# Stores of a hybrid recurrent layer issued from ScalarE's DMA queue instead of SyncE's

## The chip, the cores and the metric

One core of a Trainium2 chip. The metric is the device time of one execution, in microseconds (us). Engines are called as in the profile: PE is TensorE (PEld its weight loads), DVE is VectorE, ACT is ScalarE, POOL is GpSimd, SP is SyncE, which computes nothing and issues DMAs. A DMA is issued by an instruction in an engine's queue, and that queue runs in order: an issue that waits holds up everything behind it on its engine. SPq in the profile is SP's queue.

## What is computed

One layer of a decoder with four groups of recurrent heads, all in float32: 2048 prompt tokens with 16 learned tokens in front, and 8 sample sequences of 4 tokens, which start from their own states.

```python
def _layer(x, st, lw, lb, prefix):
    u = jnp.einsum('btd,de->bte', x, lw['w_in'])             # 1024 -> 3340 columns
    (z_a, xbc, dt_raw, z_b, u_b, z_c, qkv, b_raw, a_raw,
     z_d, q_d, f_d, i_d) = _split_last(u, _IN_SIZES)
    xbc, c_ssd_new = _causal_conv(xbc, c_ssd, ...); xbc = jax.nn.silu(xbc)
    y, s_ssd_new = _with_prefix(_ssd_chunked, (xs, dt, a, bm, cm), s_ssd, prefix, SSD_CHUNK)
    y_a = _rms_heads(y + d * xs, ...) * jax.nn.silu(z_a)       # A: Mamba-2 SSD
    y5, s5r_new, s5i_new = _s5_scan(u_b, ...)                # B: complex diagonal scan
    y_b = glu(jax.nn.gelu(y5)) * jax.nn.silu(z_b)
    qkv, c_gdn_new = _causal_conv(qkv, c_gdn, ...); qkv = jax.nn.silu(qkv)
    o, s_gdn_new = _with_prefix(_gdn_chunked, (l2norm(q), l2norm(k), v, beta, g), s_gdn, ...)
    y_c = _rms_heads(o, ...) * jax.nn.silu(z_c)              # C: gated delta rule
    o, s_hg_new = _with_prefix(_hgrn_chunked, (silu(q_d), k_h, i_d, logf), s_hg, ...)
    y_d = _rms_heads(o, ...) * jax.nn.silu(z_d)              # D: HGRN2
    out = jnp.einsum('btc,cd->btd', concat(y_a, y_b, y_c, y_d), lw['w_out'])
    return _layernorm(DN_ALPHA * x + out, lw['ln_g'], lw['ln_b']), states
```

The input x goes through a layer norm first. Outputs are the layer's y of prompt and samples and the seven final states of each.

## The kernel before

The 2096 tokens are 17 chunks: chunk 0 holds the 16 learned tokens and the 32 sample tokens, the others 128 prompt tokens each. The projections run over two halves (chunks 0 to 8 and 9 to 16) in blocks of up to 384 or 512 tokens. A product in float32 accuracy is three: high part times high part, high times low, low times high (xh and xl, the two halves of w).

- `phase1a` (one per half): layer norm and transposition of x into xh and xl, and the products that are wanted token-major: u of branch B, and i (the values of branch D) with the gates' inputs. A result goes from PSUM (pj) into a tile zs by ACT (L88 in the profile is a helper through which ACT's and DVE's operations of this phase go), and a DMA stores it to u_d or v_d (L463).
- `phase1b` runs through `proj`: some 25 weight tiles of 128 columns for each half. `wload` (L578 to 580) loads one tile into wr, ACT makes the high part of w (L579) and POOL the low part. Each block of products is taken up by the tile's consumer. `conv_tile` copies it to raw (L635), forms the causal convolution cv on POOL and DVE (L639, L641) and its SiLU on ACT (L652), in a tile acc that is normalised later, or in a tile zs that is stored at once to qkv_d or xbc_d (L654). `stream_out` has ACT write a function of the block to zs (L813 to L827) and stores it to z_d (the gates z) or qfk_d (q, f and k of branch D) at L804.
- zs has two buffers, shared by all of these; pj has two buffers in PSUM, pq, for all other products, six. raw, cdec and the other tiles have theirs.
- All else are jobs, generators that `poll` weaves between the products: the gates (g_g, L521; te, dtte), the conv tiles' l2 norm (sq, L681 to L683; l2r), `c_pre` with its decays (rows_d is loaded into cdec, POOL subtracts at L725, ACT exponentiates at L727, DVE multiplies into cma at L753), the constants of branch B (cosT, sinT, bui, L956 to L961; bs_wt, the sum of L1070 and L1071 at L1072; bs_cl loaded at L1042), and `d_group` of branch D, whose output is copied by ACT to d_oy (d_oya, d_oyb; L1703) and stored to od_d (L1704).
- Behind the second half's tiles come the chunks of branches C and A (a_L is the decay of A, L725 to L727), `rms` (f_sq, L1752; f_h), and for every chunk the gating and the product with w_out (woh and wol are its high and low parts, L1816 and L1817), the closing layer norm and the store of y.

The order of PE's instructions is the one in which the kernel is written out, with the jobs woven in by fixed times. On the other engines a scheduler orders the instructions by its own model of the times, except in a few chains that are kept in order. It also gives every DMA one of eight completion semaphores (DMAHW0 to DMAHW7) in rotation, in the order of issue over all queues; a DMA waits until the one before it on its semaphore has landed. In the kernel before all 1047 DMAs are issued by SP: `self.ld` for loads and `self.st` for stores are the same function, `nc.sync.dma_start`.

Of the kernel before, what the change touches and what calls it, by code (L numbers as in the profile page):

```python
# [62 lines left out]
def tof(t):  # L63
    return HEAD + 128 * (t - 1) if t else 0
# [6 lines left out]
class Pinned:  # L71
    """An engine whose instructions don't move ahead of earlier ones."""
# [8 lines left out]
class Chain:  # L81
    """An engine whose instructions issued through here stay in the order in which they are written."""
# [14 lines left out]
class Kern:  # L97
# [8 lines left out]

    def pool(self, name, bufs, **kw):
        return self.tc.tile_pool(name=name, bufs=bufs, reuse_waits="tile", **kw)

    # The tensor engine runs in the order in which the kernel is written out. Dependent chains  # L110
    # are generators ("jobs") that yield the time until their next step can start; they are
    # woven between the matrix products of the projections.
# [64 lines left out]
    # ---------------------------------------------------------------- constants  # L177
    def consts(self, cp):
        nc, V, S, G = self.nc, self.V, self.S, self.G
        a = self.a  # L180
# [13 lines left out]
        # sums the two parts of 32 channels of a head  # L194
# [24 lines left out]
    # ---------------------------------------------------------------- phase 1  # L219
    def small_loads(self, cp):  # L220
        """Job: small parameters, and the conv histories of the sample sequences channel-major."""
        a, V = self.a, self.Vp
        yield 8.2
        # channel-major small parameters, through one transpose
# [29 lines left out]
        # HGRN2 lower bound: softmax over the single layer, cumulative sum minus the first entry  # L254
# [70 lines left out]
    def phase1a(self, half, xp):  # L325
        """Layer norm and transposition of the input, and the products whose results are wanted token-major.
        The first yield comes before anything that needs the space of xh, xl or the weight ring."""
# [46 lines left out]
        def weights(i, parts):  # L374
            """u | i, dt, a, b: high and low parts."""
# [23 lines left out]
        else:  # L399
            # the first tile waits for as little as possible: one row comes by DMA, the other through the tensor engine  # L400
# [35 lines left out]
        for q, j in sorted(((q, j) for q in range(len(seq)) for j in (0, 1)), key=lambda x: x[0] + lag * (x[1] != half)):  # L436
# [26 lines left out]
            self.st((self.v_d if j else self.u_d)[tof(t):tof(t) + n], uv[:n, 0:256])  # L463
# [18 lines left out]
    def gates_in(self, half, sp):  # L482
# [3 lines left out]
        o = 1 - half          # chunk 0, the tail, is the first of half 0  # L486
# [14 lines left out]
        # softplus = max(x, 0) + log1p(e), log1p(e) = 2 atanh(e / (2 + e))  # L501
# [20 lines left out]
        # beta = sigmoid  # L522
# [1627 lines left out]
```

## Time and profile before

| | |
|---|---|
| time, three runs | 1446.28, 1452.7, 1456.98 us; median 1452.7 |
| profiled execution: span (its only time) | 1448.2 us |
| granted clock of PE, mean | 0.936 of full speed |
| PE busy | 1294.9 us, 89% |
| DVE, ACT, POOL busy | 934.2, 536.1, 616.3 us |
| DMA traffic | 195.79 MB, 135 GB/s in the mean |

The busy times are sums over the whole span, and the stages differ: a stretch is read in the table by stretch, and what an engine waited for in its list of waits. PEclk is the clock that was granted to TensorE, 1.00 at 2.4 GHz and 0.5 at 1.2 GHz; a mean between them is a mix of the two. A line number is that of the kernel before; in the changed kernel all lines from 107 on are two further down.

### The profile page before, as it was taken

The numbers are of one execution on the slowest core, as the hardware profiler recorded it, in microseconds if no ns is written. First come the engines' busy times: TensorE is split into PE (matmuls) and PEld (weight loads), VectorE is DVE, ScalarE is ACT, GpSimd is POOL, SyncE is SP. The second block draws the span as 40 slices with busy tenths as digits, with TensorE's granted clock in tenths as the row PEclk, the third lists the DMA queues.
The fourth block names the chain that finished last, engine by engine and source line by source line (L and its number), as shares of the span: only waits on it lengthen the run. The fifth ranks groups of instructions, "written<-read, shape, count | busy, mean of one in ns | idle before, by whom it ended". The sixth has DMA issues, their size and how long they took to land. (4 is left out here: it accounts for less than half of the span.)

```text
span 1448.2 us, 23800 instructions
## 1 busy us (share of the span) xinstructions
PE 1294.9 (89%) x8596; PEld 1090.3 (75%) x8596; DVE 934.2 (65%) x2173; ACT 536.1 (37%) x1010; POOL 616.3 (43%) x508
## 2 busy tenths in 40 slices
PE   7984898899898999998996888789997999999997
PEld 6974788878877999877674677677775677777776
DVE  8899524557978549474355789962345676665654
ACT  3224256545214342353543442242434332333211
POOL 4065322524433312152434443441324476676665
PEclk9997999999989999999998899899998899999999
DMA  8511552464337434215534633125649777676333
GB/s 211 192 49 36 127 143 57 140 189 114 106 97 203 145 104 153 77 39 158 157 87 121 201 102 95 44 88 145 177 124 251 196 198 190 198 182 184 111 105 113
DMA packets 259007, 195.79 MB, mean 135 GB/s; under 512 B 70950, under 2 KB 231928, under 8 KB 258873
## 3 DMA queue, kind: packets, MB, share of 16 engines
q1 hardware_dynamic: 258890, 194.28, 47.2%
q8 instruction: 68, 1.11, 0.3%
q14 instruction: 49, 0.39, 0.1%
HBM read 125.01 MB, written 64.31 MB: 131 GB/s over the span
## 5 line engine op out<-in xcount | busy, mean ns | idle before, releaser
L126 PE MATMUL pj<-xh,w 128*128 128x384 f32 (+2 forms) x1760 | 547.8, 379 | 10.8 <-ACT raw L635 5.5
L126 PEld LDWEIGHTS pj<-xh,w 128*128 128x128 f32 x1760 | 339.7, 200 | 57.4 <-issue 11.6
L126 PE MATMUL pj<-xl,w 128*128 128x384 f32 (+2 forms) x880 | 322.8, 367 | 0.0
L126 PEld LDWEIGHTS pj<-xl,w 128*128 128x128 f32 x880 | 176.3, 200 | 12.4 <-issue 0.5
L580 POOL TENSOR_TENSOR w<-wr,w 128x1024 fp32r<-128x1024 f32 x44 | 109.9, 2497 | 85.6 <-ACT w L579 68.0
L641 DVE SCALAR_TENSOR_TENSOR cv<-raw,par,cv 128x384 f32<-128x384 f32 (+2 forms) x150 | 130.5, 872 | 9.5 <-POOL cv L639 8.2
L126 PE MATMUL pj<-woh,o_mh 128*128 128x512 f32 (+2 forms) x280 | 116.6, 416 | 6.3 <-DVE xt L1846 3.2
L126 PE MATMUL pj<-wol,o_mh 128*128 128x512 f32 (+2 forms) x280 | 109.4, 391 | 6.2 <-POOL wol L1817 5.9
L126 PE MATMUL pj<-woh,o_ml 128*128 128x512 f32 (+2 forms) x280 | 109.4, 391 | 0.0
L126 PE MATMUL pj<-w,xh 128*128 128x256 f32 (+3 forms) x544 | 105.2, 295 | 0.0
L639 POOL TENSOR_SCALAR cv<-raw,par 128x384 f32<-128x384 f32 (+2 forms) x50 | 49.3, 986 | 119.0 <-ACT raw L635 95.4
L126 PEld LDWEIGHTS pj<-w,xh 128*128 128x128 f32 (+1 forms) x544 | 84.6, 189 | 1.2 <-ACT xh L88 0.8
L126 PE MATMUL pj<-w,xl 128*128 128x256 f32 (+3 forms) x272 | 78.0, 291 | 0.8 <-DVE xl L88 0.8
L725 POOL TENSOR_TENSOR cdec<-cdec,negm 128x256 f32<-128x256 f32 x32 | 29.4, 921 | 98.6 <-DMA cdec<-rows_d 63.1
L126 PEld LDWEIGHTS pj<-woh,o_mh 128*128 128x128 f32 (+1 forms) x280 | 52.3, 187 | 18.6 <-DVE xt L1846 4.0
L126 PEld LDWEIGHTS pj<-wol,o_mh 128*128 128x128 f32 (+1 forms) x280 | 52.5, 188 | 16.0 <-POOL wol L1817 6.9
L1789 DVE TENSOR_TENSOR y<-y,f_R 128x768 f32<-128x768 f32 (+1 forms) x17 | 27.1, 1591 | 56.0 <-POOL f_R L1788 50.9
L126 PEld LDWEIGHTS pj<-woh,o_ml 128*128 128x128 f32 (+1 forms) x280 | 52.2, 187 | 12.3 <-issue 0.7
L308 POOL TENSOR_TENSOR lnrs<-lnve,mhalf 128x1 f32<-128x1 f32 (+1 forms) x34 | 24.5, 720 | 74.0 <-DVE lnve L88 46.2
L813 ACT ACTIVATE zs<-pj 128x384 f32<-128x384 f32 (+2 forms) x40 | 20.8, 520 | 87.6 <-PE pj L126 72.8
L126 PEld LDWEIGHTS pj<-w,xl 128*128 128x128 f32 (+1 forms) x272 | 51.2, 190 | 1.5 <-DVE xl L88 1.3
L1788 POOL TENSOR_TENSOR f_R<-f_R,f_z 128x768 f32<-128x768 f32 (+1 forms) x17 | 30.2, 1778 | 51.1 <-DMA f_R<-r_d 32.5
(570 smaller groups left out, 2687.8 us busy)
## 6 DMA issues: line engine op xcount, KB each, us to landing
wr<-in_w_in_dram SPq DMA_DIRECT2D x46, 512.0 KB
xt<-in_x_prompt_dram SPq DMA_DIRECT2D x16, 512.0 KB
xn_d<-xt SPq DMA_DIRECT2D x16, 512.0 KB
ma<-cma SPq DMA_DIRECT2D x64, 128.0 KB
xt<-xn_d SPq DMA_DIRECT2D x16, 512.0 KB
out_dram<-xt SPq DMA_DIRECT2D x15, 512.0 KB
f_R<-r_d SPq DMA_DIRECT2D x32, 192.0 KB
cdec<-rows_d SPq DMA_DIRECT2D x32, 128.0 KB
```

Of the source, the lines that this page charges most:

```text
L126: self._pe(self.PE.matmul(out, lhsT, rhs, start=start, stop=stop, **kw), 0.01 + n * (1 if rhs.dtype == F32R else 4) / 2400)
L308: self.G.tensor_tensor(rs[:n], ve[:n], self.mhalf[:n, 0:1], ALU.pow)
L580: self.G.tensor_tensor(w[:, :, 1], raw, w[:, :, 0].bitcast(F32), SUB)
L639: G.tensor_scalar(cv[:, 0:m], raw[:, 3:3 + m], w[3], b, op0=MUL, op1=ADD)
L641: V.scalar_tensor_tensor(cv[:, 0:m], raw[:, k:k + m], w[k], cv[:, 0:m], op0=MUL, op1=ADD)
L725: G.tensor_tensor(d[:n, :, :n], d[:n, :, :n], m[:n, None, :n].to_broadcast([n, nh, n]), ADD)
L813: S.activation(z, p, AF.Silu)
L1788: G.tensor_tensor(R[:, :, :n], R[:, :, :n], z[:, :, :n], MUL)
L1789: V.tensor_tensor(y6[:, 0:6, :n], y6[:, 0:6, :n], R[:, :, :n], MUL)
```

## The change

A third function, `self.sa`, is ScalarE's `dma_start`. It takes the place of `self.st` at the stores of tiles that an ACT instruction wrote last. (The other lines of the diff remove comments.)

```diff
         self.ld = nc.sync.dma_start
         self.st = nc.sync.dma_start
 
+        self.sa = nc.scalar.dma_start
+
     def pool(self, name, bufs, **kw):
...
             S.copy(uv[:n, 0:256], p[:n, 0:256])
             if j:
                 V.tensor_copy(self.gat[:n, t, :], p[:n, 256:268])
-            self.st((self.v_d if j else self.u_d)[tof(t):tof(t) + n], uv[:n, 0:256])
+            self.sa((self.v_d if j else self.u_d)[tof(t):tof(t) + n], uv[:n, 0:256])
             if q == len(seq) - 1:
...
                 S.activation(o, cv[:, 0:n], AF.Silu)
             if nrm is None:
-                self.st(dst[:, t0:t0 + n], o)
+                self.sa(dst[:, t0:t0 + n], o)
             else:
...
             for fn, dst in outs:
                 z = self.zp.tile([128, 512], F32, name="zs")
                 fn(z[:, 0:n], p[:, 0:n])
-                self.st(dst[:, t0:t0 + n], z[:, 0:n])
+                self.sa(dst[:, t0:t0 + n], z[:, 0:n])
             if mark and t0 + n == BASE[self.half] + WID[self.half]:
...
                 oy = tp.tile([128, 2, 128], F32, name="d_oy" + sfx)
                 S.copy(oy[:, :, :n], ov[:, :, :n])
-                self.st(self.od_d[:, :, tof(t):tof(t) + n].rearrange("g p t -> p g t"), oy[:, :, :n])
+                self.sa(self.od_d[:, :, tof(t):tof(t) + n].rearrange("g p t -> p g t"), oy[:, :, :n])
                 p = self.pt()
```

These are 34 stores of u_d and v_d, 30 of qkv_d and xbc_d out of zs, 70 of z_d and qfk_d, and 16 of od_d: 150 of 1047 DMAs. 897 stay on SP, among them all loads and the stores of tiles that DVE, POOL or PE wrote last, and one of od_d for chunk 0. The bytes and the shapes are the same. ACT has as many computations as before, with the 150 issues among them; each store stands behind ACT's own write of its tile. The order on PE doesn't change at all. The scheduler places some instructions of the other engines anew: on ACT 91 of 1012 by up to 5 places, on DVE 597 by up to 17, on POOL 22 by up to 4, and of the DMAs left on SP 113 by up to 10.

**Phase 1a, SP's queue and ACT's.** Before, the stores at L463 stand on SP between loads (bs_cl, wr, x); in brackets what each waits for (Activation, DVE, PE and Pool are those engines' own progress):

```order
L271 DMA aco<-in_gdn_a_log_dram 128x4 [waits DMAHW1_49]
L271 DMA sd_691<-in_ssd_d_dram 128x4 [waits DMAHW2_49]
L1042 DMA bs_cl<-in_s_c_re_dram 128x2x64 [waits DMAHW3_49]
L1042 DMA bs_cl<-in_s_c_im_dram 128x2x64 [waits DMAHW4_49]
L463 DMA u_d<-zs 48x256 [waits DMAHW5_49,Activation_49]
L1105 DMA gluw<-in_s_glu_w_dram 128x2x256 [waits DMAHW6_49,Pool_49]
L578 DMA wr<-in_w_in_dram 128x8x128 [waits DMAHW7_49,PE_49]
L372 DMA xn_d<-xt 128x1024 [waits DMAHW0_49,DVE_49]
L339 DMA xt<-in_x_prompt_dram 128x1024 [waits DMAHW1_49,DMAHW0_49,PE_49]
L463 DMA v_d<-zs 128x256 [waits DMAHW2_49,Activation_49]
```

Now, on ACT, they stand behind the copy to zs and ahead of the next copies and of xh, the high part of x, which PE multiplies with:

```order
L88 COPY zs<-pj 128x256 [waits PE_49]
L465 DMA u_d<-zs 128x256 [waits DMAHW4_49,Activation_49]
L88 CAST xh<-pq 128x4x48 [waits PE_49] x2
L88 COPY zs<-pj 48x256 [waits PE_49]
L465 DMA u_d<-zs 48x256 [waits DMAHW6_49,Activation_49]
L88 CAST xh<-pq 128x4x128 [waits PE_49] x2
L88 COPY zs<-pj 128x256 [waits DMAHW4_49,PE_49]
L465 DMA v_d<-zs 128x256 [waits DMAHW2_49,Activation_49]
L88 COPY zs<-pj 128x256 [waits DMAHW6_49,PE_49]
L465 DMA u_d<-zs 128x256 [waits DMAHW5_49,Activation_49]
```

The u_d and v_d stores have left SP, and with them the wait for ACT in front of wr and x; on ACT they bring waits for DMAHW semaphores.

**ACT at about 100 us.** Before, the square of the l2 norm (sq, L682) stands twice ahead of raw and of the high part of a weight tile:

```order
L650 ACTIVATE acc<-cv 128x256
L682 ACTIVATE sq<-sq 128x64
L682 ACTIVATE sq<-sq 128x256
L635 COPY raw<-pj 128x384
L579 CAST w_1491<-wr 128x8x128
```

Now raw and the weights stand between the two squares:

```order
L652 ACTIVATE acc<-cv 128x256
L684 ACTIVATE sq<-sq 128x64
L637 COPY raw<-pj 128x384
L581 CAST w_1491<-wr 128x8x128
L684 ACTIVATE sq<-sq 128x256
```

raw (L637 now) and w (L581 now) have moved one square forward.

**DVE at about 140 us.** Before, four steps of the rotation cosT, sinT (L957, L959) stand ahead of the third sum bs_wt (L1072), which PE transposes next:

```order
L1070 TENSOR_TENSOR bs_wt<-bs_X,bpr 128x128
L957 TENSOR_TENSOR bs_l<-sinT,bui 128x256
L959 TENSOR_TENSOR sinT<-cosT,bui 128x16x16 x2
L957 TENSOR_TENSOR bm_1371<-bui 128x16
L959 TENSOR_TENSOR bvi<-bur,bui 128x16
L571 COPY g_rs<-pq 16x128
L641 SCALAR_TENSOR_TENSOR cv<-raw,par,cv 128x384
L626 COPY raw<-hist 128x8x3
L627 MEMSET raw 128x3
L1072 TENSOR_TENSOR bs_wt<-bs_wt,bs_wu 128x512
```

Now the sum comes first and the four steps (L959 and L961 in the new numbers) behind it:

```order
L958 TENSOR_TENSOR bvr<-bur 128x16
L573 COPY g_rs<-pq 16x128
L643 SCALAR_TENSOR_TENSOR cv<-raw,par,cv 128x384
L1074 TENSOR_TENSOR bs_wt<-bs_wt,bs_wu 128x512
L628 COPY raw<-hist 128x8x3
L629 MEMSET raw 128x3
L959 TENSOR_TENSOR bs_l<-sinT,bui 128x256
L961 TENSOR_TENSOR sinT<-cosT,bui 128x16x16 x2
L959 TENSOR_TENSOR bm_1371<-bui 128x16
L961 TENSOR_TENSOR bvi<-bur,bui 128x16
```

The steps L957 and L959 of before have moved behind the sum; the conv step cv in front of it is the same.

**ACT at about 1100 us.** Before, the square f_sq of `rms` stands behind three of four exponentials of a_L:

```order
L813 ACTIVATE zs<-pj 128x512
L815 ACTIVATE zs<-zs,par 128x512
L727 ACT_TABLE_LOAD
L727 ACTIVATE a_L<-a_L,nac 128x128 x3
L1752 ACTIVATE f_sq<-f_sq 128x768
L727 ACTIVATE a_L<-a_L,nac 128x128
```

Now it stands ahead of them and of the load of their function table, behind the store of the gate:

```order
L815 ACTIVATE zs<-pj 128x512
L817 ACTIVATE zs<-zs,par 128x512
L806 DMA z_d<-zs 128x512
L1754 ACTIVATE f_sq<-f_sq 128x768
L729 ACT_TABLE_LOAD
L729 ACTIVATE a_L<-a_L,nac 128x128 x4
```

f_sq (L1754 now) comes next in the after order, with no a_L in front of it.

## Rows read from the trace of the kernel before

**Rows 1.** Page: busy us of each engine (share of the span) and instructions

```profile
PE 1294.9 (89%) x8596; PEld 1090.3 (75%) x8596; DVE 934.2 (65%) x2173; ACT 536.1 (37%) x1010; POOL 616.3 (43%) x508
```

**Rows 2.** Table by stretch: length, busy us (instructions) PE PEld DVE ACT POOL, PEclk, DMA share, GB/s

```profile
50.00:100.00 50.00, 46.41 (x358) 45.27 (x356) 47.60 (x230) 15.41 (x34) 17.79 (x26) 1.00 0.34 114
100.00:150.00 50.00, 26.82 (x144) 24.09 (x142) 48.27 (x148) 20.94 (x41) 30.10 (x33) 0.80 0.11 29
```

**Rows 3.** PE's waits: waiting line, what ended it: us in total, times, longest us

```profile
PE pq L120 <- DVE bs_wt L1072: 13.3, 3, 8.3
...
PE pq L126 <- ACT Qa L1635: 6.3, 5, 2.6
...
PE pj L126 <- ACT raw L635: 5.5, 2, 3.1
...
PE pq L120 <- DMA bs_cl<-in_s_c_re_dram: 2.3, 1, 2.3
```

**Rows 4.** SP's waits, same columns, at the four kinds of store

```profile
SPq L654 <- ACT zs L652: 80.7, 16, 10.5
...
SPq L463 <- ACT zs L88: 42.8, 18, 5.6
...
SPq L804 <- ACT zs L815: 37.6, 15, 5.5
...
SPq L1704 <- ACT d_oya L1703: 22.2, 9, 3.5
```

**Rows 5.** Page, costliest groups: count | busy us, mean ns | idle before, releaser

```profile
L126 PE MATMUL pj<-xh,w 128*128 128x384 f32 (+2 forms) x1760 | 547.8, 379 | 10.8 <-ACT raw L635 5.5
...
L725 POOL TENSOR_TENSOR cdec<-cdec,negm 128x256 f32<-128x256 f32 x32 | 29.4, 921 | 98.6 <-DMA cdec<-rows_d 63.1
```

**Rows 6.** Issues of two kinds of store: duration ns min/median/max, first and last start

```profile
L463 SPq DMA_DIRECT2D u_d<-zs x17: 319/330/457, 22.4 to 608.0; - x17
...
L804 SPq DMA_DIRECT2D qfk_d<-zs x30: 319/376/1328, 184.6 to 814.6; - x30
```

**Rows 7.** ACT's waits, columns as in rows 3

```profile
ACT zs L813 <- PE pj L126: 72.8, 27, 7.5
```

**Rows 8.** SP's waits for a DMA that the issue doesn't need

```profile
SPq L578 <- DMA wr<-in_w_in_dram: 8.4, 3, 3.4
...
SPq L463 <- DMA xt<-in_x_prompt_dram: 1.9, 1, 1.9
```

**Rows 9.** Timeline of DVE around bs_wt: start us, us, engine, line, operation

```profile
124.00 5.43 DVE L641 SCALAR_TENSOR_TENSOR cv<-raw,par,cv 128x328 f32<-128x328 f32 x1
129.35 2.82 DVE L1072 TENSOR_TENSOR bs_wt<-bs_wt,bs_wu 128x512 f32<-128x512 f32 x1
...
138.10 0.41 DVE L957 TENSOR_TENSOR bs_l<-sinT,bui 128x256 f32<-128x256 f32 x1
138.43 0.75 DVE L959 TENSOR_TENSOR sinT<-cosT,bui 128x256 f32<-128x256 f32 x2
139.10 0.71 DVE L957 TENSOR_TENSOR bm<-bui 128x16 f32<-128x16 f32 x1
...
140.65 0.67 DVE L1072 TENSOR_TENSOR bs_wt<-bs_wt,bs_wu 128x512 f32<-128x512 f32 x1
```

**Rows 10.** Timeline of PE's weight loads; in brackets the idle time before and its releaser

```profile
102.57 0.19 PEld L126 LDWEIGHTS pj<-xh,w 128*128 128x128 f32 x1 [2.67 <-ACT raw L635]
...
114.98 0.50 PEld L126 LDWEIGHTS pq<-g_g,triu 128*128 128x128 f32 x2 [7.75 <-DVE g_g L521]
...
132.23 0.71 PEld L120 LDWEIGHTS pq<-ident,bs_wt 128*128 128x128 f32 x4 [8.66 <-DVE bs_wt L1072]
...
141.43 0.42 PEld L120 LDWEIGHTS pq<-ident,bs_wt 128*128 128x128 f32 x4 [4.26 <-issue]
```

**Rows 11.** The same timeline around 1100 us

```profile
1103.84 0.24 PEld L126 LDWEIGHTS pq<-f_h,sel 128*32 128x32 f32 x16 [3.43 <-DVE f_h L1756]
...
1118.86 0.15 PEld L126 LDWEIGHTS pj<-woh,o_mh 128*48 128x48 f32 x1 [3.20 <-ACT woh L1816]
```

## The prediction

> **What bounds the kernel now.** I read the head of the page first. TensorE (PE) is busy for 1294.9 of 1448.2 us, 89%; VectorE (DVE) 65%, GpSimd (POOL) 43%, ScalarE (ACT) 37% [rows 1]. So PE sets the time, and only its 153 us of idle time (1448.2 - 1294.9) and the clock that falls behind a stall are to be had.
>
> Then the table by stretch. From 50 to 150 us it is another engine that limits: DVE is busy 47.6 and 48.27 us of 50, while PE drops to 26.82 us between 100 and 150, at a granted clock of 0.80 [rows 2]. That row also gives the price of a stall. PE is idle there for 23.2 us; a mean of 0.80 between the levels 1.2 and 2.4 GHz (0.5 and 1) is 40% of the stretch, 20 us, at 1.2 GHz, which loses up to 10 us more. One us of stall then costs up to (23.2 + 10) / 23.2 = 1.4 us. I use 1.4 for any stall that comes or goes.
>
> Third, PE's waits. The longest end with DVE (bs_wt 13.3 us in 3); the two largest groups that end with ACT are 6.3 us in 5 and 5.5 us in 2, and the only one that ends with a DMA is 2.3 us in 1 [rows 3]. SP's own waits look quite different: four of its groups, all of stores that now move, come to 80.7 + 42.8 + 37.6 + 22.2 = 183.3 us in 58 waits [rows 4]. The question of this case is whether that large number is in anyone's way.
>
> **The change part by part.**
>
> *Removed from SP's queue: 150 issues and their waits for ACT.* PE's program is the same instruction by instruction, so nothing is saved or added on PE itself; only what it waits for can move. What stands behind a store on SP is the next load. If those loads were what PE, or an engine that PE waits for, lacked, waits on a DMA would show. PE has 2.3 us of them [rows 3]. That one is real: the loads of bs_cl were held on SP just before, and they can now come earlier. But it lies at 89 us, in the stretch where DVE is at 47.6 of 50 us, and PE only meets DVE sooner. POOL does wait for loads of rows_d ahead of cdec, 63.1 us in 32 operations [rows 5], but the store ahead of such a load holds it for a few us of a wait that has another cause (the load must wait for rows_d itself), and PE's work goes on beside it. Bounds for earlier loads: 0, and -3 us from the 2.3 us at 1.4. I take **-1**, nearer to the end that rows show, since there are some other held loads behind whose consumers PE has a small wait.
>
> *Added to ACT: the issue time.* On SP one issue takes 319 to 457 ns for u_d and 319 to 1328 ns for qfk_d, medians 330 and 376 [rows 6]. If ACT pays the same, 150 x 0.33 to 0.38 is 50 to 57 us. ACT has 1448.2 - 536.1 = 912 us to spare, but an issue is on the path where something that PE wants stands right behind it. Mostly nothing does: the store follows the copy zs, and ACT then waits for PE's next block (72.8 us in 27 waits at L813 alone, 2.7 us in the mean, 7.5 at most) [rows 7]. The other end: an issue of 0.35 us in front of each of the seven waits that end with ACT [rows 3], times 1.4, is 3.4 us. I take a third of that, **+1**, and 0 to +3 for the range.
>
> *Added to ACT: waiting for other transfers.* Every DMA waits for the one that had its completion semaphore eight DMAs earlier, whichever queue that was in. On SP this was hidden among waits for data; now 102 of the 150 stores carry such a wait in ACT's queue, next to the compute instructions. What the trace shows of such waits, for a transfer that the waiting one has no use for, is 8.4 us in 3 at the weight load L578, and 1.9 us in 1 at a store of this change itself, L463: 10.3 us in 4, 2.6 us each [rows 8]. All other groups of the kind in SP's list are no longer than 1.5 us. Queued behind the store are zs of the next block, raw of a conv tile, the decay cdec and the high parts of the weights, w. A block of 128x384 is 24 products of some 0.38 us [rows 5], 9 us, and PE has two buffers for them, so a wait of 2.6 us in front of zs or raw is covered. In front of a step of a chain it isn't. Bounds: 0, and half of those 10.3 us times 1.4, +7; I take **+1**, near the lower end, since ACT would wait for PE at most of these places anyway [rows 7].
>
> *Buffers.* zs has two buffers, so a store that leaves SP's queue sooner frees one sooner for ACT. PE has its own two buffers in front of that, and no row shows PE waiting for a zs for long. Nothing.
>
> *Moved: the order on ACT, DVE and POOL.* This is the part with a sign. (a) On DVE the four steps L957 and L959, which took 0.41, 0.75 and 0.71 us in their three longer rows [rows 9], now stand behind the third bs_wt sum instead of in front of it. The PE stall that this sum ends is 4.26 us [rows 10]; it comes down by 1.9 us, or by up to 2.9 us with one more conv step that moves. But DVE has to do the moved steps all the same, in a stretch that it fills; the fourth sum comes earlier by about 1.4 us, and that is what is left at the end of the stretch. (b) On ACT raw and the weight copy come ahead of a square that held them: the stall of 2.67 us goes, but the next one, 7.75 us for g_g, ends when DVE is ready, and that isn't sooner [rows 10]. Nothing. (c) At 1100 us the square f_sq comes ahead of the three exponentials of a_L: some 2 of the 3.43 us go; then PE stands 3.20 us later anyway for the output weights, woh, whose load isn't moved [rows 11]. Nothing. Together **-1.4**, between 0 and 2.9 x 1.4 = -4.
>
> Sum: -1 + 1 + 1 - 1.4 = -0.4 us against the profiled span of 1448.2 us, the only time of that execution. The span is 4.5 us under the median of the three runs, 1452.7, so I set the sum on the median: 1452.3, **1452 us**.
>
> One thing that I can't price from the order: from 124.00 us one conv step on DVE lasts 5.43 us and the next bs_wt sum 2.82 us, where the same sum took 0.67 us later [rows 9]; both lie beside long additions on POOL, and the wait of 8.66 us at 132.23 is mostly theirs [rows 10]. Such a meeting depends on fractions of a us. The order around it is unchanged, so I leave it; but it can go (-7 us) or come elsewhere (+7).
>
> *A rule that speaks against the change.* An issue takes 0.33 us on SP [rows 6], an engine that computes nothing here. The Trainium skill, "DMA: Bandwidth & Descriptors", section "Issuing engines are not separate DMA queues", says that DMAs of all issuing engines run on the same 16 DMA engines, and that issuing from several saves only the sequencer's time to start them, which is usually small. By that alone the change would save SP the 50 to 57 us above, which hold nothing up, and give 1452.7. SP's 183.3 us [rows 4] are more than issue time, since the queue waits in order; whether that is worth anything is the first rival's question.
>
> **The rivals.**
>
> *Faster: SP's queue was in the way after all.* For it: 183.3 us of holds [rows 4], and POOL's 63.1 us in front of cdec [rows 5], from which a chain runs over ACT and DVE to PE. Of PE's 153 us of idle time some 33 are at the start and between 100 and 150; if the loads took a sixth of the other 120, that is 20 us, x 1.4 = 28 us: 1425 us. Against it: PE's one wait on a DMA [rows 3].
>
> *Slower: ACT stands where SP stood.* For it: 102 stores wait for a transfer that is not theirs, at 2.6 us each where it is felt [rows 8], and it is now the engine that feeds PE's inputs that stands. If a third of them are felt on ACT, 34 x 2.6 = 88 us, and a quarter of that reaches PE through a chain step, 22 us, x 1.4 = 31 us: 1484 us. It decides from about 10 us of new PE stalls (14 us with the clock). Against it: on SP only four such waits are long enough to be seen [rows 8], and the two product buffers cover 9 us. Should the issue also last longer on ACT than on SP, since both engines now start transfers at once, this rival gains: 150 x 0.3 us more, 45 us on ACT, a quarter of it on PE is 11 us.
>
> *The change frees nothing.* Loads on SP still wait for the completion semaphores of the stores that went to ACT: the loads that stood behind a store now wait for it to land. Then SP's 183.3 us come back under another name, and PE sees nothing: 1453 us, inside my forecast.
>
> **How the numbers follow.** A change of 1% (14.5 us) is about what the runs of this kernel can tell, as the three shown spread over 10.7 us. My forecast, with the rival that nothing is freed in it: 0.74. Faster rival 0.14, slower rival 0.12. Inside the forecast the bounds are -3 - 4 = -7 and +3 + 7 = +10 around 1452.7, 1446 to 1463; with the 7 us of a meeting that moves either way 1439 to 1470; with 2 us more on the low side, where the rival has the larger chance and reaches in with its small cases, 1437 to 1470. Below and above lie about 0.1 each, the rest of the two rivals. Faster by over 1% 0.14, within 1% 0.74, slower by over 1% 0.12.
>
> **What would show it in the profile after.** SP's waits for zs and d_oya are gone from its list, and PE's busy time is as before, near 1295 us. ACT's count of computations is about the same, and its queue shows waits for DMAs at L465, L656, L806 and L1706 (the new numbers of the lines) of less than 30 us in all; PE's waits that end with ACT stay under 35 us. Between 100 and 150 us DVE is still at 48 of 50, the third bs_wt stall is down to 1 to 3 us, and g_g still holds PE for 7 us or more. I am wrong if PE's idle time moves by more than 10 us outside of that stretch, or if the loads of rows_d, qkv_d or qfk_d land several us earlier and a PE stall goes with them.

## The result and the profile after

| | before | after |
|---|---|---|
| time, median | 1452.25 us (4 runs, 1446.28 to 1456.98) | 1469.42 us (4 runs, 1460.28 to 1476.69) |
| ratio, 95% interval | | 1.013 (1.0095 to 1.0164) |
| profiled execution: span, granted clock | 1448.2 us, 0.936 | 1472.3 us, 0.922 |

The changed kernel is slower by 1.3%. The forecast was no change, 1452 us, with 0.12 for slower by over 1%; 1469 us lies at the upper end of its range of 1437 to 1470 us.

The head of the page of the changed kernel, and from its costliest groups and its DMA queues (q10 is ACT's queue):

```profile
PE 1315.0 (89%) x8596; PEld 1105.3 (75%) x8596; DVE 938.5 (64%) x2173; ACT 538.2 (37%) x1010; POOL 615.4 (42%) x508
...
q1 hardware_dynamic: 235402, 166.42, 41.0%
q10 hardware_dynamic: 23488, 27.86, 5.6%
...
L128 PE MATMUL pj<-xh,w 128*128 128x384 f32 (+2 forms) x1760 | 557.7, 385 | 8.7 <-ACT raw L637 4.3
...
L727 POOL TENSOR_TENSOR cdec<-cdec,negm 128x256 f32<-128x256 f32 x32 | 29.3, 920 | 95.5 <-DMA cdec<-rows_d 49.6
```

The first thing to see is PE's busy time: the same 8596 instructions took 1315.0 us instead of 1294.9 [rows 1], 20.1 us of the 24.1 us that the span grew. PE was idle for 1472.3 - 1315.0 = 157.3 us instead of 153.3. A product of the same shapes lasts 385 ns in the mean instead of 379 [rows 5], and the granted clock is 0.922 instead of 0.936. So in these two profiles most of the time went into products at the lower clock. How much of that is the change and how much the two executions that were profiled is looked at below, with the clocks of all runs. The second thing is that the loads did come sooner in one place that the faster rival named: the part of POOL's wait for cdec that ends with a load of rows_d fell from 63.1 to 49.6 us [rows 5]. But POOL's whole idle time in front of cdec fell by 3.1 us only, from 98.6 to 95.5: it waits for something else now. PE's time shows nothing of it.

SP's and then ACT's waits in the changed kernel (columns as in rows 3):

```profile
SPq L778 <- DMA qkv_d<-zs: 9.7, 3, 3.7
```

```profile
ACT xh L88 <- DMA xt<-in_x_prompt_dram: 4.2, 1, 4.2
ACT xh L88 <- DMA bs_l<-in_s_lam_im_dram: 4.1, 1, 4.1
...
ACT zs L815 <- DMA xt<-in_w_in_dram: 2.6, 1, 2.6
```

The issues at L806 and L465 (as in rows 6):

```profile
L806 ACTq DMA_DIRECT2D qfk_d<-zs x30: 326/326/812, 189.0 to 830.1; - x30
```

```profile
L465 ACTq DMA_DIRECT2D u_d<-zs x17: 326/326/337, 20.9 to 621.8; - x17
```

SP's waits for an ACT write of zs, 183.3 us in four groups [rows 4], are gone. A new wait has come: SP's small loads at L778 (L776 before), which read acc from ma, waited 9.7 us for stores of qkv_d, which they don't read. And ACT waits for loads that it doesn't need, 4.2, 4.1 and 2.6 us. The issue itself costs 326 ns on ACT in the median; on SP it was 330 and 376 ns [rows 6].

PE's weight loads with the idle time before them (as in rows 10):

```profile
45.49 0.30 PEld L128 LDWEIGHTS pj<-w,xh 128*128 128x128 f32 x2 [1.66 <-ACT xh L88]
...
118.92 0.50 PEld L128 LDWEIGHTS pq<-g_g,triu 128*128 128x128 f32 x2 [7.56 <-DVE g_g L523]
...
136.40 0.71 PEld L122 LDWEIGHTS pq<-ident,bs_wt 128*128 128x128 f32 x4 [9.25 <-DVE bs_wt L1074]
144.38 0.42 PEld L122 LDWEIGHTS pq<-ident,bs_wt 128*128 128x128 f32 x4 [1.93 <-issue]
...
1123.01 0.24 PEld L128 LDWEIGHTS pq<-f_h,sel 128*32 128x32 f32 x16 [1.91 <-DVE f_h L1758]
...
1139.24 0.15 PEld L128 LDWEIGHTS pj<-woh,o_mh 128*48 128x48 f32 x1 [4.36 <-ACT woh L1818]
```

At the places that the prediction had looked at, the order did what it said: the stall behind the third bs_wt sum is down from 4.26 to 1.93 us [rows 10], g_g still holds PE for 7.56 us, f_h came down from 3.43 to 1.91 us and woh gave most of it back, 4.36 instead of 3.20 us [rows 11]. PE gets through the products that it does between 100 and 150 us in the kernel before 0.9 us sooner than there (1.6 us in the changed kernel's second profile, after_again below). The loss lies at other places.

### The profile page after: what moved, and what is told of

Read it like the earlier page. It is cut to its first block, busy times and chain, and to the rows that moved or that the text cites. A ratio compares the mean times of both kernels' runs of the same rounds, so it can differ in the third digit from the quotient of the medians.

```text
span 1472.3 us, 23743 instructions
## 1 busy us (share of the span) xinstructions
PE 1315.0 (89%) x8596; PEld 1105.3 (75%) x8596; DVE 938.5 (64%) x2173; ACT 538.2 (37%) x1010; POOL 615.4 (42%) x508
## 4 chain that ended last, share of the span: by engine, by line
PE 28%; DVE 19%; DMA 9%; issue 6%; POOL 6%; ACT 3%; SPq 1%; POOLq 0%; ACTq 0%; DVEq 0%
PE pj L128 17%; PE pq L128 10%; DVE cv L643 3%; DMA f_R<-r_d 2%; DVE Qa L1668 2%; DVE cdec L789 2%; PE pq L122 2%; DMA r_d<-f_rs 1%; DVE acc L791 1%; POOL f_R L1790 1%; DVE d_ATa L1672 1%; POOL xt L1867 1%; POOL xt L1868 1%; DMA b<-b 1%; DVE xt L88 1%
## 5 line engine op out<-in xcount | busy, mean ns | idle before, releaser
L128 PE MATMUL pj<-xh,w 128*128 128x384 f32 (+2 forms) x1760 | 557.7, 385 | 8.7 <-ACT raw L637 4.3
L128 PEld LDWEIGHTS pj<-xh,w 128*128 128x128 f32 x1760 | 348.0, 204 | 56.6 <-issue 11.2
L128 PE MATMUL pj<-xl,w 128*128 128x384 f32 (+2 forms) x880 | 328.8, 374 | 0.0
L128 PEld LDWEIGHTS pj<-xl,w 128*128 128x128 f32 x880 | 180.5, 205 | 12.9 <-issue 0.5
L643 DVE SCALAR_TENSOR_TENSOR cv<-raw,par,cv 128x384 f32<-128x384 f32 (+2 forms) x150 | 122.1, 815 | 9.5 <-POOL cv L641 8.2
L727 POOL TENSOR_TENSOR cdec<-cdec,negm 128x256 f32<-128x256 f32 x32 | 29.3, 920 | 95.5 <-DMA cdec<-rows_d 49.6
L128 PE MATMUL pq<-Qa,d_ka 128*128 128x128 f32 (+2 forms) x256 | 37.1, 289 | 18.2 <-DVE Qa L1668 16.8
```

What stands on the lines that cost most here:

```text
L128: self._pe(self.PE.matmul(out, lhsT, rhs, start=start, stop=stop, **kw), 0.01 + n * (1 if rhs.dtype == F32R else 4) / 2400)
L643: V.scalar_tensor_tensor(cv[:, 0:m], raw[:, k:k + m], w[k], cv[:, 0:m], op0=MUL, op1=ADD)
L727: G.tensor_tensor(d[:n, :, :n], d[:n, :, :n], m[:n, None, :n].to_broadcast([n, nh, n]), ADD)
```

## The experiments

**Two things changed at once: the queue and the order.** PE's order is the same, but the scheduler placed the other engines' instructions anew. To part the two, a kernel can be held to the order of another one: each engine's instructions get an edge to the one that stood before them there (an edge for the order of issue alone, which adds no wait).

```diff
+def _follow(nc, tc):
+    by = {i.name: i for i in nc.cur_bb.bb.instructions}
+    for text in _ORDER:      # one list for each engine
+        at, prev = 0, None
+        for d in text.split():
+            at += int(d)
+            i = by.get("I-%d" % at)
...
+            if prev is not None:
+                tc.add_manual_dep(i, prev, mybir.DependencyInfo(
+                    mybir.DependencyClass.NoSync, mybir.DependencyReason.DATA), reason="order")
+            prev = i.name
...
         Kern(tc, a, o).run()
+        _follow(nc, tc)
```

The theories: Q, the queue costs (ACT stands at issues and at foreign transfers); O, the new order costs; C, the clock falls by small shifts and every kernel draws its own lot.

`act_oldorder`: the changed kernel with `_follow` in the order of the kernel before.

> The 150 stores are on ACT's queue as in the changed kernel, but the computations of DVE, ACT and POOL and the DMAs left on SP are held in the order of the kernel before. Theory Q (the queue: issues and waits among ACT's computations make PE's stalls longer, and the clock falls behind them): near the changed kernel, ratio 1.010 to 1.016 to the kernel before. Theory O (it is the order that the scheduler placed anew, above all on DVE): near the kernel before, 0.997 to 1.003. Theory C (the clock falls here and there by small shifts, and any shift gives a draw): anywhere between 0.995 and 1.016, with 188 to 235 us at the lower clock.

`sp_neworder`: the kernel before with `_follow` in the order of the changed kernel.

> All stores on SP's queue as before, but the computations of DVE, ACT and POOL and SP's 897 other DMAs are held in the order of the changed kernel. Theory Q: near the kernel before, 0.997 to 1.003. Theory O: near the changed kernel, 1.010 to 1.016. Theory C: anywhere between, not related to the other run.

`before_again` and `after_again`: the two kernels themselves.

> The kernel before once more: ratio 0.998 to 1.002 by Q and O, and a profile with about 188 us at the lower clock and 148 us idle on PE (Q and O: the falls of the clock repeat in the same places). By C the falls repeat only behind long stalls, and the sum at the lower clock moves by 20 us or more.

> The changed kernel once more: ratio 1.010 to 1.016, and by Q and O a profile with about 234 us at the lower clock; by C a sum that is 20 us or more away from that.

| kernel | stores on | order | ratio to before | 95% interval | span, PE busy of the profile |
|---|---|---|---|---|---|
| before_again | SP | before | 0.998 | 0.9954 to 1.0005 | 1448.4, 1294.0 |
| act_oldorder | ACT | before | 1.0069 | 1.0041 to 1.0098 | 1464.0, 1303.4 |
| sp_neworder | SP | after | 1.0112 | 1.0065 to 1.0159 | 1472.0, 1308.0 |
| after_again | ACT | after | 1.0107 | 1.0067 to 1.0147 | 1468.5, 1303.8 |

With no store moved at all, the new order alone makes the kernel as slow as the change did. The queue alone, in the old order, costs 0.7%. The two don't add up: with the new order, the queue costs nothing that can be measured.

Theory C needs a closer look, because the profiles alone mislead. The two of the changed kernel differ by 11 us in PE's busy time, and by 27 us in the time at 1.2 GHz (234 and 206 us), which is what theory C had forecast; the two of the kernel before differ by 5 us only (188 and 183 us). But every run lists its mean granted clock, not only the profiled one. The profiles of the kernel before have 0.936 and 0.937, near the top of the 0.925 to 0.938 of the 23 runs of that kernel that were measured along with these. An estimate of what the clock costs goes by its two levels: a mean clock of c over a time t is 2(1 - c)t at 1.2 GHz, and up to half of that is lost.

| kernel | mean clock of its runs | of the kernel before | us longer, mean of runs | of these by the clock (estimate) | more idle on PE in the profile, us |
|---|---|---|---|---|---|
| act_oldorder | 0.930 | 0.930 | 10.1 | 1.9 | 7.3 |
| sp_neworder | 0.929 | 0.930 | 16.2 | 3.7 | 10.7 |
| after_again | 0.929 | 0.930 | 15.3 | 3.4 | 11.4 |

So the clock isn't the main cause in these three: they run at nearly the same clock as the kernel before, and PE stands idle for longer. What is left without the clock's part, 8 to 12.5 us, is uncertain by 3 to 4.5 us. The 20 us of additional busy time in the first pair of profiles came mostly from an execution of the kernel before with a high clock and one of the changed kernel with a low one.

**What of the queue costs.** The same kernel in the order of before, with a part of the stores on ACT.

```diff
 # act_old_uv: this one line; act_old_nouv: the other three
-            self.st((self.v_d if j else self.u_d)[tof(t):tof(t) + n], uv[:n, 0:256])
+            self.sa((self.v_d if j else self.u_d)[tof(t):tof(t) + n], uv[:n, 0:256])
 # act_old_zqod: z, q, f, k and od_d
-                self.st(dst[:, t0:t0 + n], z[:, 0:n])
+                self.sa(dst[:, t0:t0 + n], z[:, 0:n])
...
 # act_old_qkv: i >= 4; act_old_xbc: i < 4
-                self.st(dst[:, t0:t0 + n], o)
+                (self.sa if i >= 4 else self.st)(dst[:, t0:t0 + n], o)
```

`act_old_uv`:

> Only the 34 stores of u_d and v_d are on ACT's queue; everything else on SP, and all computations and other DMAs in the order of the kernel before. If the queue costs where ACT stands at a foreign transfer in front of xh (the store of u_d at 44 us waited 4.3 to 4.7 us for a load of x in all three profiles with these stores on ACT): ratio 1.002 to 1.005, with PE 2 to 4 us later at the place that is at 50 us in the kernel before, and nothing else. If the queue's cost lies in the other stores: 1.000.

`act_old_nouv`:

> The other 116 stores (conv tiles, z, q, f, k, od_d) on ACT's queue, u_d and v_d on SP, all in the order of the kernel before. If the cost of the queue is that of the phase 1a stores: 0.999 to 1.003. If it is the issues and waits in general: 1.004 to 1.007, spread over the whole span.

`act_old_zqod`:

> Only the stores of z, q, f, k and od_d (86) on ACT's queue; u_d, v_d and the conv tiles' stores on SP, all in the order of the kernel before. With the 30 conv stores on ACT, SP's row of 30 small loads (L778) waited 5.9 us for qkv_d stores to land, the next load of weights was issued later, and PE came 5 us late between 350 and 378 us. If that coupling through the completion semaphores is the main cost of the queue besides phase 1a: these 5 us are gone, ratio 0.999 to 1.003. If the issues on ACT cost in general: 1.003 to 1.005.

`act_old_qkv`:

> Only the 10 stores of qkv_d are on ACT's queue, all else on SP and in the order of the kernel before. If the conv stores' cost is the coupling of the two queues through the completion semaphores (SP's small loads of L778 wait for these stores to land, the weights' load stands behind): ratio 1.002 to 1.006, with SP waiting 5 us or more for qkv_d stores and PE some 5 us late between 350 and 378 us. If ACT's issues and waits in general: a third of the 0.55% of the conv stores or less, 1.000 to 1.002.

`act_old_xbc`:

> Only the 20 stores of xbc_d on ACT's queue, otherwise as the one above. Coupling: 0.998 to 1.002 and nothing lost between 350 and 378 us. Issues and waits in general: two thirds of the conv stores' 0.55%, 1.002 to 1.005.

| kernel | stores on ACT | ratio to before | 95% interval |
|---|---|---|---|
| act_old_uv | 34 | 1.0017 | 0.9987 to 1.0047 |
| act_old_nouv | 116 | 1.0045 | 1.0017 to 1.0074 |
| act_old_zqod | 86 | 0.9989 | 0.9963 to 1.0016 |
| act_old_qkv | 10 | 1.002 | 0.999 to 1.0049 |
| act_old_xbc | 20 | 1.0011 | 0.9983 to 1.0038 |

More than half of the moved stores, those of z, q, f, k and od_d, cost nothing: ACT's 86 issues have room, as the prediction said. The 30 conv stores are the difference of act_old_nouv and act_old_zqod, 0.56%, uncertain by 0.4%. What the 34 others cost, and what the 10 and the 20 cost alone, lies inside the uncertainty, so their places are read from the traces. The first is ACT's timeline of act_old_uv:

```profile
40.54 0.37 ACT L88 COPY zs<-pj 128x256 f32<-128x256 f32 x1 [2.45 <-PE pj L127]
44.91 0.33 ACTq L464 DMA_DIRECT2D u_d<-zs  x1
45.27 1.07 ACT L88 CAST xh<-pq 128x512 fp32r<-128x512 f32 x2 [4.36 <-DMA xt<-in_x_prompt_dram]
```

zs was written by 40.91. Its store could be issued only at 44.91, when a load of x that had its completion semaphore before had landed; xh, which PE needs, stood behind it. This is the very store that had waited 1.9 us on SP [rows 8]; there xh didn't stand behind it. PE's stall behind it is the one of 1.66 us in the changed kernel above, and after_again, act_oldorder and act_old_uv have it too (1.5 to 1.9 us on PE, at 44 us). The product that PE starts at 50.0 us in the kernel before starts 2.2 to 4.4 us later in the five profiles with these stores on ACT, and at most 1.3 us later in the others. In the whole time, 0.17%, it is not more than the runs can tell.

The second goes the other way round. SP's timeline around the 32 small loads, first of the kernel before, then of act_old_qkv:

```profile
333.81 0.50 SPq L654 DMA_DIRECT2D qkv_d<-zs  x1
334.35 11.35 SPq L776 DMA_DIRECT2D acc<-ma  x28
345.79 0.82 SPq L654 DMA_DIRECT2D qkv_d<-zs  x2
346.71 0.40 SPq L578 DMA_DIRECT2D wr<-in_w_in_dram  x1
```

```profile
335.59 0.78 SPq L777 DMA_DIRECT2D acc<-ma  x2
336.46 0.82 SPq L756 DMA_DIRECT2D ma<-cma  x2
337.33 17.75 SPq L777 DMA_DIRECT2D acc<-ma  x30
355.18 0.40 SPq L579 DMA_DIRECT2D wr<-in_w_in_dram  x1
```

SP's waits, ACT's, DVE's and PE's timelines of act_old_qkv:

```profile
SPq L777 <- DMA qkv_d<-zs: 8.8, 3, 3.3
```

```profile
359.36 1.04 ACT L580 CAST w<-wr 128x1024 fp32r<-128x1024 f32 x1 [1.18 <-DMA wr<-in_w_in_dram]
...
375.30 0.52 ACT L653 ACTIVATE zs<-cv 128x384 f32<-128x384 f32 x1 [4.90 <-DVE cv L642]
375.73 0.46 ACT L636 COPY raw<-pj 128x384 f32<-128x384 f32 x1
```

```profile
356.77 0.19 DVE L788 TENSOR_TENSOR cdec<-acc 128x31 f32<-128x31 f32 x1 [1.21 <-DMA acc<-ma]
...
370.68 2.60 DVE L642 SCALAR_TENSOR_TENSOR cv<-raw,par,cv 128x384 f32<-128x384 f32 x1
```

```profile
376.24 0.44 PE L127 MATMUL pj<-xh,w 128*128 128x384 f32 x1 [2.74 <-ACT raw L636]
```

In the kernel before, SP waits until ACT has written the tile, issues the store and goes on. Now the small loads, which use all eight completion semaphores in turn, must wait until the store on ACT has been issued and has landed: 17.75 us for 30 loads instead of 11.35 for 28, and the load of the next weights is issued at 355.18 instead of 346.71. ACT waits 1.18 us for these weights and DVE 1.21 us for the small loads themselves. PE then stalls for 2.74 us at a place where it had not stalled. act_old_xbc has neither this wait nor this stall, and act_old_zqod hasn't either; act_old_nouv has both (8.4 us, 2.77 us). The coupling is not all of that stall: raw, which ends it, stands on ACT behind a zs that waits for DVE, and there one step of cv took 2.60 us (0.66 in the kernel before), until POOL had finished an instruction beside it. What 10 against 20 stores cost in total, 0.2% and 0.1%, can't be told apart from each other or from nothing.

In the new order the wait is still there, 9.7 and 11.5 us in the changed kernel's two profiles, but it costs PE little. The products that PE does between 350 and 378 us in the kernel before take 28.1 us there, 31.3 to 33.7 us in the three kernels with the qkv_d stores on ACT in the order of before, and in the new order 29.3 and 30.1 us with them on ACT against 29.6 us on SP (sp_neworder). That is a part of why the queue's cost isn't seen on top of the new order.

**What of the order costs.** One pair of instructions on ACT first.

```diff
 # sp_wlate: the kernel before, held in its own order but for this pair on ACT;
 # after_wearly: the changed kernel with the pair the other way round
-L579 CAST w_3098<-wr 128x8x128
 L826 ACTIVATE zs<-pj 128x384
+L579 CAST w_3098<-wr 128x8x128
```

`sp_wlate`:

> All stores on SP and everything in the order of the kernel before, but for one pair: the high part of one weight tile on ACT stands behind the third zs of the f tile, as in the changed kernel, and not ahead of it. If that pair makes PE's stall at 284 us longer (zs waits for a store to land, the weights behind it, POOL's low part and its l2r behind those): PE 2 to 4 us later at the place that is at 300 us in the kernel before, ratio 1.001 to 1.003. If the stall comes from elsewhere: no difference there.

`after_wearly`:

> The changed kernel in its own order, but for the same pair put back: the weights ahead of the third zs. If the pair is the cause, the 2 to 3.6 us that the changed kernel loses between 275 and 300 us go, ratio to the kernel before 1.007 to 1.012 instead of 1.010 to 1.013; if not, they stay.

ACT's timeline of the kernel before, then ACT's, POOL's, DVE's and PE's of sp_wlate:

```profile
276.64 1.04 ACT L579 CAST w<-wr 128x1024 fp32r<-128x1024 f32 x1
280.46 0.49 ACT L826 ACTIVATE zs<-pj 128x384 f32<-128x384 f32 x1 [2.78 <-DMA qfk_d<-zs]
```

```profile
284.99 0.49 ACT L826 ACTIVATE zs<-pj 128x384 f32<-128x384 f32 x1 [3.90 <-DMA qfk_d<-zs]
285.37 1.04 ACT L579 CAST w<-wr 128x1024 fp32r<-128x1024 f32 x1
```

```profile
286.49 2.37 POOL L580 TENSOR_TENSOR w<-wr,w 128x1024 fp32r<-128x1024 f32 x1 [6.58 <-ACT w L579]
288.81 3.22 POOL L695 TENSOR_TENSOR l2r<-l2r,mhalf 128x18 f32<-128x18 f32 x1
```

```profile
292.07 0.18 DVE L697 TENSOR_SCALAR l2r<-l2r 128x18 f32<-128x18 f32 x1 [6.21 <-POOL l2r L695]
```

```profile
292.39 0.37 PE L120 MATMUL pq<-ident,l2r 128*18 128x128 f32 x1 [4.14 <-DVE b L1140]
```

zs has two buffers, so the third zs must wait for a store to land. Ahead of it the weights cost nothing; behind it they wait 3.9 us with it, POOL's low part waits for them, l2r stands behind it on POOL and gets its last step on DVE, and PE waits 4.14 us for that, where it had waited 1.16 us in the kernel before (1.41 us in that kernel's second profile). The changed kernel has the pair in this order and a stall of 3.05 us there. With the pair put back (after_wearly) it is 1.35 us:

```profile
289.49 0.27 PE L122 MATMUL pq<-ident,l2r 128*18 128x128 f32 x1 [1.35 <-DVE b L1142]
```

One swap of two neighbours gave 3.0 us of stall to the one kernel and took 1.7 us from the other. The products that PE does between 250 and 300 us in the kernel before take 50.0 us there and 55.1 us in sp_wlate, 54.5 and 53.0 us in the changed kernel and 50.1 us in after_wearly. In the whole time it is not seen: sp_wlate 1.0013 (0.9988 to 1.0039), after_wearly 1.0109 (1.007 to 1.0148). Against after_wearly's shorter stalls stands its clock: a mean of 0.923 over its six runs (0.919 to 0.925), against 0.929 in after_again. Why the clock fell is open. sp_wlate is also the control for `_follow`: a kernel held to the order of before, all but this pair, is as fast as that kernel.

The order in parts, and other orders. `sp_newdve`:

> All stores on SP; DVE's and POOL's computations in the order of the changed kernel, ACT's and SP's in the order of the kernel before. If most of what the order costs comes from DVE's 597 moved instructions: ratio 1.006 to 1.011, with the losses at 200 to 225 (b_fs), 825 to 850 (cma) and 1175 to 1200 us. If it comes from ACT's 91: 0.999 to 1.004, with the loss at 275 to 300 us gone as well.

`sp_ord_zq` and `sp_ord_conv`:

> All stores on SP, but the computations in the order that the scheduler makes when only z, q, f and k go to ACT's queue (170 instructions of DVE, 59 of ACT, 24 of POOL moved). If the order of the kernel before is simply better than others that the same scheduler makes: 1.003 to 1.011. If only the changed kernel's own order is bad, at a few places: 0.998 to 1.003.

> The same with the order that it makes when only the conv tiles' stores go to ACT's queue (270 instructions of DVE, 35 of ACT, 19 of POOL moved): the same two answers.

`sp_ord_od` and `sp_ord_uv`:

> All stores on SP, the computations in the order that the scheduler makes when only the 16 stores of od_d go to ACT's queue (61 instructions of DVE, 28 of ACT, 13 of POOL moved). If any other order of this scheduler is worse than that of the kernel before: 1.003 or more. If the loss grows with the number of moved instructions: 0.999 to 1.003.

> The same with the order that it makes when only u_d and v_d go to ACT's queue (344 instructions of DVE, 38 of ACT, 10 of POOL moved): 1.003 to 1.016 by both; 0.998 to 1.002 if the losses of the two other orders were accidents of theirs.

```diff
 # the kernel before, all stores on SP, and in _ORDER the lists of
 # sp_newdve: the changed kernel for DVE and POOL, the kernel before for ACT and SP
 # sp_ord_x: a kernel in which only the stores x are issued by ACT, for DVE, ACT and POOL
         Kern(tc, a, o).run()
+        _follow(nc, tc)
```

| kernel, all stores on SP | moved on DVE, ACT, POOL | ratio to before | 95% interval | span, PE busy of the profile |
|---|---|---|---|---|
| sp_neworder | 597, 91, 22 | 1.0112 | 1.0065 to 1.0159 | 1472.0, 1308.0 |
| sp_newdve | 597, 0, 22 | 1.0059 | 1.0035 to 1.0082 | 1464.5, 1304.5 |
| sp_ord_zq | 170, 59, 24 | 1.0157 | 1.0119 to 1.0196 | 1483.5, 1319.0 |
| sp_ord_conv | 270, 35, 19 | 1.0085 | 1.0056 to 1.0114 | 1468.1, 1304.0 |
| sp_ord_od | 61, 28, 13 | 1.0057 | 1.0032 to 1.0083 | 1460.2, 1304.3 |
| sp_ord_uv | 344, 38, 10 | 1.0011 | 0.9982 to 1.004 | 1445.3, 1302.8 |

DVE's and POOL's new order make about half of the loss. The other half lies with ACT's 91 instructions and with SP's DMAs, whose order sp_neworder takes from the changed kernel too. One place on DVE can be read from the traces, first of the kernel before, then of sp_newdve, with PE's stall:

```profile
1183.69 0.40 DVE L1461 TENSOR_TENSOR c_vb<-c_vb,pq 128x256 f32<-128x256 f32 x1
...
1187.16 1.23 DVE L1789 TENSOR_TENSOR y<-y,f_R 128x768 f32<-128x768 f32 x1
```

```profile
1202.02 3.13 DVE L1789 TENSOR_TENSOR y<-y,f_R 128x768 f32<-128x768 f32 x1 [1.67 <-POOL f_R L1788]
...
1206.54 0.40 DVE L1461 TENSOR_TENSOR c_vb<-c_vb,pq 128x256 f32<-128x256 f32 x1
```

```profile
1207.08 1.08 PE L126 MATMUL pq<-c_vb,c_N 128*128 128x64 f32 x8 [1.93 <-DVE c_vb L1461]
```

In the new order the product with f_R, for which DVE must wait on POOL, stands ahead of c_vb, which PE needs. The five profiles with DVE's new order have this stall (1.1 to 2.1 us), the nine with the order of before have none.

Of the five orders that the same scheduler made for slightly different kernels (sp_newdve is a mixture), four are slower than that of the kernel before and none is faster. In sp_ord_zq the clock does make the larger part: 0.920 in the mean of its six runs against 0.929, some 16 of its 25 us by the same estimate. So a new order can cost by longer stalls and by the clock, and theory C holds for a part of these kernels. The loss doesn't grow with the number of instructions that moved: 61 on DVE cost 0.6%, 344 cost nothing. ACT's new order alone wasn't tried: together with DVE's old one, the two engines would wait for each other.

## Why the prediction was wrong

*The step that failed is "Moved: the order on ACT, DVE and POOL", -1.4 us (-4 to 0).* With all stores on SP, it measured +1.1%, 16 us at 1452. What was said of its places held, as the profile after shows: PE is 0.9 and 1.6 us sooner through the stretch from 100 to 150 us. The mistake was the choice of the places. I had followed those where a step that PE waits for came forward, and took the rest of 597 and 91 moved instructions for nothing. Among the rest are pairs in which a step that PE's chain needs now stands behind one that waits. w behind zs at 285 us is one on ACT, where zs waits for a store to land, and cost 3.0 us of stall in sp_wlate; c_vb behind the product with f_R at 1187 us is one on DVE, 1.1 to 2.1 us. In all PE was idle for 10.7 us more in sp_neworder, which at the prediction's own 1.4 makes 15 of the 16 us. The bound "not above 0" had no reason in the trace.

*The price of a stall, 1.4,* is not what failed. Seven of the other kernels have over 6 us more of idle time on PE in their profiles. Six of them lost 0.9 to 1.5 us for each of these by their ratios at 1452 us (act_oldorder 1.4, sp_neworder 1.5), and sp_ord_zq, with the lowest clock, 2.0. It isn't a constant, though: after_wearly lost 1.1% with 2 us less of idle time in its profile. Taken from the spans of single profiles the price comes out higher (23.8 us for 10.7 in sp_neworder), because the profiled execution of the kernel before had a high clock.

*The queue's own terms, -1 + 1 + 1 (-3 to +10),* were too low as well. With the order held, the queue cost 0.7%, 10 us (6 to 14). Waiting on ACT for other transfers measured 4.2 + 4.1 + 2.6 = 10.9 us in the changed kernel, much as the 10.3 us from which the bound was made, and in the stores of phase 1a it makes PE 2 to 4 us late. What the sum didn't have is the other direction, loads on SP that wait for stores on ACT. The slower rival put the price at 31 us with ACT standing in a third of 102 stores; that isn't what happened, though the sign was right.

*"The change frees nothing".* This rival had SP's loads wait for the stores' completion, and said that PE sees nothing of it. Half of that was right: SP waits for qkv_d stores to land, 8.4 to 11.5 us in every kernel with the qkv_d stores on ACT. But with the order held PE does see it: the 30 conv stores make 1.0045 against 0.9989 without them.

*Issue time, +1 (0 to +3).* Right: 326 ns on ACT, and 86 stores with 0.9989.

*Earlier loads, -1.* POOL's wait for rows_d ahead of cdec fell by 13.5 us, its idle time there by 3.1 us, and PE gained nothing that shows. PE's wait for bs_cl at 93 us grew from 2.3 to 4.1 us, and that goes with the order: it is 4.3 us in sp_neworder, with all stores on SP. No run shows a gain beyond its interval.

*The meeting of DVE and POOL at 124 us.* I put most of the 8.66 us at bs_wt down to it, and that holds; what didn't hold is that it depends on fractions of a us. In the changed kernel other instructions meet. DVE's timeline, then POOL's:

```profile
128.41 4.38 DVE L552 TENSOR_TENSOR dtte<-sp,te 128x36 f32<-128x36 f32 x1 [0.57 <-ACT te L549]
132.72 2.35 DVE L960 TENSOR_TENSOR bvr<-bvr,bm 128x16 f32<-128x16 f32 x1
135.00 0.55 DVE L643 SCALAR_TENSOR_TENSOR cv<-raw,par,cv 128x328 f32<-128x328 f32 x1
...
135.67 0.67 DVE L1074 TENSOR_TENSOR bs_wt<-bs_wt,bs_wu 128x512 f32<-128x512 f32 x1
```

```profile
127.54 5.21 POOL L1063 TENSOR_TENSOR Pw<-Pw,bs_w 128x2304 f32<-128x2304 f32 x1
132.71 2.33 POOL L582 TENSOR_TENSOR w<-wr,w 128x1024 fp32r<-128x1024 f32 x1
```

The conv step and the sum are short now, but dtte, which took 0.18 us in the kernel before, takes 4.38 us and ends with POOL's addition, and the next step ends with POOL's low part of w. The sum stands behind both, and PE waits 9.25 us for it. Every one of the 18 profiles has such a pair there; with the order of before it is the prediction's pair each time, 5.4 and 2.8 us.

*The rule of the Trainium skill* ("DMA: Bandwidth & Descriptors", section "Issuing engines are not separate DMA queues"), that issuing from several engines saves only issue time, held here for the gain: the kernel with 86 stores on ACT is at 0.9989. It says nothing of the loss, in which the two queues were bound to each other by their completion semaphores and the order had changed.

What stays open: why all of the queue's 0.7% is lost in the new order, which other pairs make up the rest of the 1.1%, and why some orders have a lower clock. Several places are known by their longer stalls, but only one was tried alone, and it is too small to be seen in the time.

## What to carry to other kernels

A change of an issuing engine under an automatic scheduler is two changes, and the second, the order, can be the larger. Hold the order fixed to see the first, and give the new order to the old kernel to see the second; and count in a forecast that the order of a tuned kernel can get worse when it is drawn again: here four of five orders did, and none got better. A single profile is one draw of the clock: compare the clocks of all runs before a difference in busy time is put down to a change. With few completion semaphores in rotation over two queues, a DMA on one queue waits for whatever the other has issued eight before: a store that waits for a computation then holds up loads on the other engine until it has landed.

## What the runs showed of the hardware that was not expected

The clock also falls in a stretch where PE doesn't wait. Between the same two PE instructions, 177 of them, before and in the changed kernel (columns as in rows 2):

```profile
1000.00:1025.10 25.10, 25.05 (x177) 16.97 (x175) 11.99 (x28) 9.70 (x20) 7.97 (x9) 0.93 0.77 198
```

```profile
1017.60:1045.80 28.20, 28.15 (x177) 18.45 (x175) 12.08 (x28) 9.84 (x20) 8.84 (x9) 0.82 0.76 189
```

PE is idle for 0.05 us in both, and the stretch lasts 3.1 us longer at a clock of 0.82 instead of 0.93, between the levels 1.2 and 2.4 GHz. Both profiles of the changed kernel have the longer form and both of the kernel before the shorter; act_old_qkv and act_old_xbc have the longer form with the order of before, act_old_zqod the shorter. What decides it was not found.

The other thing is how long DVE can be held beside POOL: dtte, 128x36, took 4.38 us, until POOL's addition ended, and 0.18 us where nothing met it. How long it lasted was set by the instruction on POOL, not by its own size.
